# Two more groups of the second down block by seven products, their weight sums formed in HBM by adding transfers

## The chip, the cores and the metric

The kernel runs on one core of one Trainium2 chip. The metric is the device time of one execution in microseconds (us). The core has a matrix engine (PE, TensorE), a vector engine (DVE), a scalar engine (ACT), GpSimd (POOL), a sequencer that mostly issues transfers (SP), and 16 DMA engines which all queues share. On-chip memory (SBUF) and the matmul accumulators (PSUM, eight banks of 128 x 512 float32) are managed by hand; weights lie in HBM.

## The reference

One transformer block in float32 on 256 rows of width 2048: three kinds of attention side by side, gated and merged, then a feed-forward part. Cut to the part that matters here:

```python
x = x + merged @ w_out[l]
h2 = rms_norm(x, g_ffn[l])
u = causal_depthwise_conv(h2 @ w_up[l], conv_w[l], conv_b[l])   # 2048 -> 2 x 5632
u_gate, u_val = jnp.split(u, 2, axis=-1)
x = x + (jax.nn.silu(u_gate) * u_val) @ w_down[l]               # 5632 -> 2048
```

The last product, of the activations a = silu(u_gate) * u_val (256 x 5632) with w_down (5632 x 2048), is the "down" product. The change is there.

## The kernel before

**Float32 by three passes.** A float32 operand is split into a high part (`hi`, a rounded copy made by ACT) and a low part (`lo`, the rest, by DVE); `three` issues three matmuls, hi x hi, lo x hi, hi x lo. So each weight tile is loaded into a `raw` buffer by SP, cast by ACT into one of four `hi` buffers and subtracted by DVE into one of four `lo` buffers (`parts`, lines 354 and 355; `piece`, lines 142 to 144, does it in the up stage), then used by PE (lines 360 to 362, and 1289 and 1290 in the up stage). In the up stage `raw` has four buffers, in the down stage six that take turns (`raw_tile`), and two small ones (`junk`) for tiles of half size.

**Stages.** After attention, gates and the output product comes the up stage (h2 @ w_up): 11 rounds of four column tiles of the gate half (`s` = 0) and then the same four of the value half (`s` = 1), each over 16 row tiles, two at a time. A `tick()` follows each pair of row tiles: it advances generators that put side work into the program, among them the convolutions (`conv`, `taken`), which end in `split_to`, that writes an activation tile into `aT`. Generators in the list `background` are advanced first in each tick, and beside the up stage one of them, `pair_sums_ahead`, forms sums of weights.

**The down product by eight or by seven.** The down product runs as two blocks of 1024 output columns (`nb` 0 and 1, function `blocked`). A block goes over the 44 row tiles of w_down in 22 groups of two (a group is a pair `p` of tiles). For one group the product is a 2 x 2 block product: two halves of the rows of x (t), two row tiles of weights (j), two column halves of 512 (n). `eight(p)` makes the eight block products directly: two loads of 512 KB. `seven(p)` makes them by a scheme of Strassen's kind with seven: it needs sums of activations (`s_of`, four of them, S1 to S4) and sums of weights T1 to T4, where, with the weight blocks B00, B01 (first row tile) and B10, B11 (second), T1 = B00 + B01, T3 = B01 + B11, T2 = T1 + B11, T4 = T2 + B10. Y, four more PSUM banks, collects products that belong to more than one output; `gather` adds them up after the last seven of the block.

The plan of a block is a string in `d_plans`: `e` a group by eight, `s` the next group by seven, `f` a step `form()` that forms the sums of activations of one pair: DVE adds and subtracts into a scratch tile (lines 369 to 374), then ACT and DVE split the four results (lines 376 and 378). Groups by seven take pairs 0, 1, 2 and so on, groups by eight the remaining ones. The first block has 11 of each, and its sums of activations are used again in the second block; there pairs from 11 on need `f` steps of their own, and their sums are written over the activations of pairs that a group by eight has just used for the last time.

**The sums of weights** are formed ahead and kept in HBM: one DRAM tile of 128 x 4 x 512 per group (`kept_for`), with the places T1, T3, T4, T2 in that order. In the up stage `pair_sums_ahead` loads the 1 MB of a pair (`pre_d`, line 305), lets DVE add (lines 252 to 254, `sums_in`), and stores 1 MB (line 295). It starts 22 ticks into the stage (`DU`) and does a pair every eight ticks; the deque `halves` lists all sums to be formed. `seven` loads, on SP in this order, B00 and T3 into one raw tile (lines 447 and 448), B10 and B11 (line 416), T1 and T2 (line 451), and T4 into a `junk` tile (line 453).

**Order.** `in_order` (keep_in_program_order) pins instructions to program order on their engine. SP issues its transfers in program order, so one that waits for a buffer holds up all behind it. POOL does nothing in the up stage but two small transfers at its start, of row scales through HBM (`rstd_row`, `rbc`, lines 1160 and 1161).

Of the kernel before, what the change touches and what calls it, by code (L numbers as in the profile page):

```python
# [10 lines left out]
F32 = mybir.dt.float32  # L11
F32R = mybir.dt.float32r
AF = mybir.ActivationFunctionType
ALU = mybir.AluOpType
AX = mybir.AxisListType

P = 128
# [16 lines left out]
PIECE = 1024  # L34
# [9 lines left out]
def hybrid_block(  # L44
# [25 lines left out]
    nc = tc.nc  # L70
    nc.scalar.preload_act_table_set("natural_log_exp_and_others")

    cst = ctx.enter_context(tc.tile_pool(name="cst", bufs=1))
# [28 lines left out]
    background = []  # L102
# [72 lines left out]
    def split_to(dst, src):  # L175

        nc.scalar.copy(dst[..., :S], src)
        nc.vector.tensor_tensor(dst[..., S:], src, dst[..., :S].bitcast(F32), ALU.subtract)
# [25 lines left out]
    def k_tiles(name):  # L204
# [23 lines left out]
    g_plans = (("", "esesesee", "esesesee"), ("esesesee", "esesesee", "esesesee"))  # L228
    d_plans = (
        "efefefef" + "sef" * 4 + "ssefsfssfssee",  # L230
        "efefef" + "sss" + "esss" * 3 + "ssee",
    )
    T1, T3, T4, T2 = range(4)
    FS2, FS4, FS3, FS1 = range(4)
    in_order = tc.keep_in_program_order
    dram = ctx.enter_context(tc.tile_pool(name="dram", bufs=1, space=bass.MemoryType.DRAM))
    by_k = lambda w: w[0].rearrange("(k p) n -> p k n", p=P)
# [6 lines left out]
        for name, w, plans in (("o", w_out, o_plans), ("d", w_down, d_plans))  # L244
        for nb, plan in enumerate(plans)
        for pr in pairs(name, plan.count("s"))
        for h in range(2)
    )

    def sums_in(w):  # L250
        both = w[:, 1:2].to_broadcast([P, 2, w.shape[2]])
        in_order(nc.vector.tensor_tensor(w[:, 0:2], w[:, 0:4:3], both, ALU.add))
        in_order(nc.vector.tensor_tensor(w[:, T2], w[:, T1], w[:, T2], ALU.add))
        in_order(nc.vector.tensor_tensor(w[:, T4], w[:, T2], w[:, T4], ALU.add))

    def kept_for(name, nb, pr):
        if (name, nb, pr) not in sums_of:
            at = f"kept_{name}{nb}_{pr}"
            sums_of[name, nb, pr] = dram.tile([P, 4, 512], F32, tag=at, name=at)
        return sums_of[name, nb, pr]  # L260
# [24 lines left out]
    def pair_sums_ahead(staging, period, add, store, most=99, delay=0):  # L285

        due = deque()
        clock = 0
        for _ in range(delay):
            yield  # L290

        def step():
            while due and due[0][0] <= clock:
                _, kept, w = due.popleft()
                in_order(nc.sync.dma_start(kept, w))

        periods = cycle(period if isinstance(period, tuple) else (period,))
        while len(halves) > 1 and halves[0][-1] == 0 and most:
            most -= 1
            name, wv, nb, pr, _ = halves.popleft()  # L300
            halves.popleft()
            kept = kept_for(name, nb, pr)
            w = staging(f"pre_{name}{nb}_{pr}")
            in_order(
                nc.sync.dma_start(
                    w.rearrange("p (k c) -> p k c", k=2), wv[:, 2 * pr : 2 * pr + 2, nb * PIECE : (nb + 1) * PIECE]
                )
            )
            w = w.rearrange("p (i c) -> p i c", i=4)
            due.append((clock + store, kept, w))  # L310
            for t in range(next(periods)):
                if t == add:
                    sums_in(w)
                step()
                clock += 1
                yield
        while due:
            step()
            clock += 1
            yield  # L320

    def first_sums():

        name, wv, nb, pr, _ = halves.popleft()
        halves.popleft()
        kept = kept_for(name, nb, pr)
        two = []
        for h in range(2):
            w = block(f"pre_{name}{nb}_{pr}_{h}").rearrange("p (i c) -> p i c", i=4)
            two.append(w)  # L330
            n0 = nb * PIECE + h * 256
            for n in range(2):
                in_order(
                    nc.sync.dma_start(
                        w.rearrange("p (k n) c -> p k n c", k=2)[:, :, n],
                        wv[:, 2 * pr : 2 * pr + 2, n0 + n * 512 : n0 + n * 512 + 256],
                    )
                )
            yield
            yield  # L340
        for w in two:
            sums_in(w)
            yield
        for _ in range(3):
            yield
        for h, w in enumerate(two):
            in_order(nc.sync.dma_start(kept[:, :, h * 256 : (h + 1) * 256], w))
            yield
# [475 lines left out]
    def in_turn(name):  # L824
        turn[0] += 1
        return staged[:, turn[0] % 2]

    background.append(pair_sums_ahead(in_turn, PF, 3, 7, most=14))
    qm = heads_of(block("qm"))
    y = norm_heads(ps, rstd, "mq")  # L830
# [237 lines left out]
    for m in range(2):  # L1068
        gate = []
        for b, plan in enumerate(g_plans[m]):  # L1070
            g, bias = [], []
# [56 lines left out]
        for n in range(2):  # L1128
            acc = gate[branches[0][3]][n]
            for i, (w, k0, nk, b) in enumerate(branches):  # L1130
# [5 lines left out]
                for t in range(NT):  # L1136
                    g = gate[b][n]
# [41 lines left out]
    for nb, plan in enumerate(o_plans):  # L1179
# [20 lines left out]
    background.append(  # L1200
        pair_sums_ahead(lambda name: ends_tile(name, F32).rearrange("p i c -> p (i c)"), 8, 1, 5, delay=DU)
    )

    def a_pair(p):
        if p < FA // 2:
            return aT[:, 2 * p : 2 * p + 2]
        if not ends:
            ends.append(ends_tile("a_ends", F32R).rearrange("p i (k c) -> p i k c", k=2))
        return ends[0][:, p - FA // 2]
# [19 lines left out]
    def y_tile(f, s):  # L1229
        return cp.tile([P, S], F32, tag="y", bufs=6, name=f"y_{f}_{s}")  # L1230

    def taken(cr, y, f, s):
        ct = s * FT + f
        u = pads[f % 2]
        ins = nc.vector.tensor_tensor(u[:, 2:], cr, rbc, ALU.mult)  # L1235
        if y is not None:
            in_order(ins)
        y = y_tile(f, s) if y is None else y
        tap = lambda j: taps[:, j, ct : ct + 1]
        nc.scalar.activation(y, u[:, 2:], AF.Identity, scale=tap(2), bias=tap(3))  # L1240
        nc.vector.scalar_tensor_tensor(y, u[:, 1 : S + 1], tap(1), y, ALU.mult, ALU.add)
        nc.vector.scalar_tensor_tensor(y, u[:, 0:S], tap(0), y, ALU.mult, ALU.add)
        if s == 0:
            nc.scalar.activation(y, y, AF.Silu)
            ys[f] = y
        else:
            g = ys.pop(f)
            nc.vector.tensor_tensor(g, g, y, ALU.mult)
            split_to(a_pair(f // 2)[:, f % 2], g)

    def conv(ps, f, s):
        taken(out_of(ps, cp.tile([P, S], F32, tag="cr", bufs=2, name=f"cr_{f}_{s}")), None, f, s)
        return
        yield
# [19 lines left out]
    for f0 in range(0, FT, 4):  # L1274
# [5 lines left out]
        for s in range(2):  # L1280
            ps = [bank(f"u{f0 + i}_{s}") for i in range(4)]
            c0 = s * D_FF + f0 * P
            for k in range(0, KT, 2):
                hi, lo = piece(upv[:, k : k + 2, c0 : c0 + 512], 2, 512, f"u{f0}_{s}_{k}")
                for j in range(2):
                    first, last = k + j == 0, k + j == KT - 1
                    for i in range(4):
                        c = slice(i * P, (i + 1) * P)
# [23 lines left out]
    N0, N1 = (plan.count("s") for plan in d_plans)  # L1312
# [3 lines left out]
    a_blocks = aT.rearrange("p k (l t q) -> p k l t q", l=2, t=NT)  # L1316
    formed = [0]

    def s_of(p, f):


        if f == FS1:
            return a_blocks[:, 2 * p, :, 1]
        if p < 9:
            return sf[:, 3 * p + f]
        if p == 9:
            return sf_more[0][:, f] if f < 2 else sf_rest[2]
        if p == 10:
            return sf[:, 27] if f == 0 else sf_rest[f - 1]
        return a_blocks[:, 2 * (p - N0 + N1) + f // 2, :, f % 2]  # L1330

    tmp_d = lambda name: place([P, PIECE], F32, "ts", name)

    def form():
        p = formed[0]
        formed[0] += 1
        if p == 9:
            sf_rest.extend(cst.tile([P, 2, P], F32R, tag=tag, name=f"sf_{tag}") for tag in ("rbc", "taps", "rows"))
        if p < 9:
            groups = [(sf[:, 3 * p : 3 * p + 3], slice(0, 3))]  # L1340
        elif p == 9:
            sf_more.append(place([P, 2, 2, P], F32R, "sf", "sf_more"))
            groups = [(sf_more[0], slice(0, 2)), (sf_rest[2], 2)]
        else:
            groups = [(s_of(p, f), f) for f in range(3)]
        pair_sums(a_pair(p), tmp_d(f"fw_{p}"), groups + [(s_of(p, FS1), FS1)])
# [4 lines left out]
    for nb, plan in enumerate(d_plans):  # L1351
        apart = [] if nb == 1 else None
        X = blocked(
            "d", w_down, nb, nb * PIECE, plan, lambda p, j: a_pair(p)[:, j], s_of, raw_d, junk,
            lambda n0, Y: gather(n0, Y, tmp_d), None, form, apart,
        )
        for t in range(NT):
            for n in range(2):
                c = nb * PIECE + n * 512
                o = xres[:, t, c : c + 512]  # L1360
                nc.vector.tensor_tensor(o, o, X[t][n], ALU.add)
                if (nb, t, n) == (1, 1, 1):
                    nc.scalar.dma_start(ov[:, t, c : c + 256], o[:, :256])
                    c, o = c + 256, o[:, 256:]
                    nc.vector.tensor_tensor(o, o, apart[0], ALU.add)
                    nc.scalar.dma_start(ov[:, t, c : c + 256], o)
                else:
                    nc.scalar.dma_start(ov[:, t, c : c + 512], o)
# [31 lines left out]
```

## Time and profile before

| | us |
|---|---|
| median of 3 runs | 1460.83 |
| lowest, highest | 1460.07, 1462.5 |
| the profiled execution's own time | 1460.56 |
| its span, first to last instruction | 1458.8 |
| granted TensorE clock, share of full | 1.00 |

| stage | from, to (us in the span) | length |
|---|---|---|
| up | 757 to 1240 | 483 |
| down, first block | 1240 to 1344 | 104 |
| down, second block | 1344 to 1455 | 111 |

The profile is of one execution. A row of a group of instructions reads: line, engine, operation, output <- input, partitions x elements and type, count | busy us, mean ns of one | idle time of that engine just before, with what ended it. A row of a stage gives busy us and count for each engine, then the granted clock, the mean busy share of the 16 DMA engines and GB/s. Matmuls are pipelined and their ends are modelled: a matmul row's own length is longer than the distance to the next one. A wait reads: who waited <- for what: us in total, times, longest. "PE u L1289" is PE's matmul into `u` at line 1289.

### The profile page before, as it was taken

To read this page: it belongs to the slowest core of one execution; us is meant where nothing else is said; L and a number is where in the kernel's file an instruction comes from. 1 tells how busy PE (TensorE), PEld (TensorE's weight loads), DVE (VectorE), ACT (ScalarE), POOL (GpSimd) and SP (SyncE) were. 2 spreads that over 40 slices of the span, in tenths; PEclk is the share of its full clock that TensorE was granted. 3 is DMA by queue.
4 is the path that set the end of the run, shared out by engine and by line. 5 is a ranking of instruction groups with operands and counts; after the bars stand their busy time and mean duration, and the time that the engine had idled before them with its cause. 6 is when DMAs were issued, how large, how long until landed. Compare 5 with 4: busy or idle time off the path is not lost.

```text
span 1458.8 us, 20569 instructions
## 1 busy us (share of the span) xinstructions
PE 1452.1 (100%) x7295; PEld 1228.4 (84%) x7295; DVE 1221.8 (84%) x1804; ACT 851.9 (58%) x1210; POOL 21.4 (1%) x52
## 2 busy tenths in 40 slices
PE   9999999999999999999999999999999999999998
PEld 7888878888888888888888888888888888888887
DVE  5788778776898899998987888888888877999878
ACT  6755445464564555546766656556556565676665
POOL 0000010010000000000000000000000000000000
PEclk9999999999999999999999999999999999999999
DMA  8797899777668576788877888888888866789896
GB/s 290 228 352 247 320 323 333 266 250 217 212 206 268 176 226 201 271 266 261 304 213 231 290 275 299 282 270 299 286 278 298 272 197 201 253 283 341 293 334 220
DMA packets 166502, 387.64 MB, mean 266 GB/s; under 512 B 12554, under 2 KB 29854, under 8 KB 162174
## 3 DMA queue, kind: packets, MB, share of 16 engines
q1 hardware_dynamic: 164702, 383.29, 79.2%
q10 hardware_dynamic: 1328, 2.11, 0.4%
q8 instruction: 57, 0.93, 0.3%
q0 software_dynamic: 368, 0.93, 0.2%
q14 instruction: 47, 0.39, 0.1%
HBM read 347.47 MB, written 38.80 MB: 265 GB/s over the span
## 4 chain that ended last, share of the span: by engine, by line
PE 95%; issue 1%; DVE 1%; DMA 1%; SPq 0%; ACT 0%; POOL 0%; DVEq 0%; POOLq 0%; ACTq 0%
PE u L1289 22%; PE u L1290 11%; PE xg L362 4%; PE xg L361 4%; PE xg L360 4%; PE xd L360 4%; PE xd L362 3%; PE xd L361 3%; PE s L362 2%; PE f L360 2%; PE s L360 2%; PE f L362 2%; PE f L361 2%; PE b L362 2%; PE s L361 2%; PE b L361 2%
## 5 line engine op out<-in xcount | busy, mean ns | idle before, releaser
L1289 PE MATMUL u<-hT,hi_u 128*128 128x512 f32 x1232 | 428.5, 394 | 0.0
L1290 PE MATMUL u<-hT,lo_u 128*128 128x256 f32 x1232 | 341.5, 277 | 0.0
L1289 PEld LDWEIGHTS u<-hT,hi_u 128*128 128x128 f32 x1232 | 231.0, 188 | 53.4
L144 DVE TENSOR_TENSOR lo_u<-raw_u,hi_u 128x1024 fp32r<-128x1024 f32 x176 | 215.5, 1225 | 72.1 <-ACT hi_u L143 71.8
L143 ACT CAST hi_u<-raw_u 128x1024 fp32r<-128x1024 f32 x176 | 184.7, 1050 | 132.7 <-PE u L1289 107.0
L1290 PEld LDWEIGHTS u<-hT,lo_u 128*128 128x128 f32 x1232 | 231.5, 188 | 0.0
L355 DVE TENSOR_TENSOR lo_d<-raw_d,hi_d 128x1024 fp32r<-128x1024 f32 x88 | 106.8, 1223 | 16.7 <-ACT hi_d L354 14.3
L354 ACT CAST hi_d<-raw_d 128x1024 fp32r<-128x1024 f32 x88 | 91.8, 1053 | 39.9 <-PE xd L361 14.3
L354 ACT CAST hi_g<-raw_g 128x1024 fp32r<-128x1024 f32 (+1 forms) x80 | 77.0, 972 | 48.5 <-PE xg L361 19.2
L355 DVE TENSOR_TENSOR lo_g<-raw_g,hi_g 128x1024 fp32r<-128x1024 f32 (+1 forms) x80 | 88.7, 1121 | 4.1 <-ACT hi_g L354 4.1
L362 PE MATMUL xg<-lo_g,xT 128*128 128x512 f32 x175 | 68.1, 389 | 0.0
L360 PE MATMUL xg<-hi_g,xT 128*128 128x512 f32 x175 | 68.1, 389 | 0.0
L361 PE MATMUL xg<-hi_g,xT 128*128 128x512 f32 x175 | 68.1, 389 | 0.0
L143 ACT CAST hi_f<-raw_f 128x1024 fp32r<-128x1024 f32 (+1 forms) x40 | 38.5, 966 | 46.3 <-PE f L361 30.7
L144 DVE TENSOR_TENSOR lo_s<-raw_s,hi_s 128x1024 fp32r<-128x1024 f32 (+1 forms) x40 | 44.5, 1119 | 24.4 <-ACT hi_s L143 24.4
L1289 PE MATMUL u<-hT_rest,hi_u 128*128 128x512 f32 x176 | 62.0, 394 | 0.0
L143 ACT CAST hi_s<-raw_s 128x1024 fp32r<-128x1024 f32 (+1 forms) x40 | 38.4, 962 | 38.2 <-PE s L361 26.5
L143 ACT CAST hi_b<-raw_b 128x1024 fp32r<-128x1024 f32 x32 | 33.7, 1052 | 45.4 <-PE b L361 18.6
L1240 ACT ACTIVATE y<-u,taps 128x256 f32<-128x256 f32 x88 | 49.5, 595 | 17.0 <-DVE u L1235 16.8
L144 DVE TENSOR_TENSOR lo_f<-raw_f,hi_f 128x1024 fp32r<-128x1024 f32 (+1 forms) x40 | 44.4, 1117 | 16.9 <-ACT hi_f L143 16.9
L360 PE MATMUL xd<-hi_d,aT 128*128 128x512 f32 x148 | 57.6, 389 | 0.0
L362 PE MATMUL xd<-lo_d,aT 128*128 128x512 f32 x148 | 57.6, 389 | 0.0
(551 smaller groups left out, 3484.0 us busy)
## 6 DMA issues: line engine op xcount, KB each, us to landing
raw_u<-in_w_up_dram SPq DMA_DIRECT2D x176, 512.0 KB, 4.8
raw_g<-in_w_in_dram SPq DMA_DIRECT2D x96, 512.0 KB, 4.5
raw_d<-in_w_down_dram SPq DMA_DIRECT2D x63, 512.0 KB, 5.6
pre_d<-in_w_down_dram SPq DMA_DIRECT2D x17, 1024.0 KB, 7.2
kept_d<-pre_d SPq DMA_DIRECT2D x17, 1024.0 KB, 6.7
raw_f<-in_w_in_dram SPq DMA_DIRECT2D x32, 512.0 KB, 5.8
raw_s<-in_w_in_dram SPq DMA_DIRECT2D x32, 512.0 KB, 6.1
raw_t_d<-kept_d SPq DMA_DIRECT2D x25, 512.0 KB, 5.8
```

The source lines that it names most:

```text
L143: pin(nc.scalar.copy(hi[:, :m], raw[:, :m]))
L144: pin(nc.vector.tensor_tensor(lo[:, :m], raw[:, :m], hi[:, :m].bitcast(F32), ALU.subtract))
L354: nc.scalar.copy(hi[:, :n], src)
L355: nc.vector.tensor_tensor(lo[:, :n], src, hi[:, :n].bitcast(F32), ALU.subtract)
L360: fix(nc.tensor.matmul(o, lhsT=ah, rhs=w[0], start=first, stop=False))
L361: fix(nc.tensor.matmul(o, lhsT=al, rhs=w[0], start=False, stop=False))
L362: fix(nc.tensor.matmul(o, lhsT=ah, rhs=w[1], start=False, stop=last))
L1240: nc.scalar.activation(y, u[:, 2:], AF.Identity, scale=tap(2), bias=tap(3))
L1289: nc.tensor.matmul(ps[i], lhsT=hi[:, j, c], rhs=hT(k + j), start=first, stop=False)
L1290: nc.tensor.matmul(ps[i][:, :S], lhsT=lo[:, j, c], rhs=hT(k + j)[:, :S], start=False, stop=last)
```

## The change

The second block's plan goes from 14 groups by seven and 8 by eight, with 3 `f` steps, to 16 and 6, with 5, in another order. The sums of weights of the two new groups, pairs 14 and 15, are not formed by `pair_sums_ahead` (its list leaves them out, and is the same 25 pairs as before for w_down), but by a new background generator of the up stage. It waits until an activation tile is being written, lets POOL copy one column of it (so that POOL waits for it on the chip), then issues on POOL a copy of the pair's 1 MB of weights from HBM into the kept tile and four transfers of 256 KB that add onto it in HBM, each of which needs the one before or the copy; 40 ticks later the same for the second pair. The places in which sums of activations of pairs 11 to 15 are kept move to the activations of pairs 16 to 19, packed without gaps.

```diff
@@ -228,8 +228,9 @@
     g_plans = (("", "esesesee", "esesesee"), ("esesesee", "esesesee", "esesesee"))
     d_plans = (
         "efefefef" + "sef" * 4 + "ssefsfssfssee",
-        "efefef" + "sss" + "esss" * 3 + "ssee",
+        "efsss" * 3 + "efssfsssssee",
     )
+    in_hbm = [("d", 1, pr) for pr in range(14, 16)]
     T1, T3, T4, T2 = range(4)
     FS2, FS4, FS3, FS1 = range(4)
     in_order = tc.keep_in_program_order
@@ -244,6 +245,7 @@
         for name, w, plans in (("o", w_out, o_plans), ("d", w_down, d_plans))
         for nb, plan in enumerate(plans)
         for pr in pairs(name, plan.count("s"))
+        if (name, nb, pr) not in in_hbm
         for h in range(2)
     )
 
@@ -318,6 +320,21 @@
             step()
             clock += 1
             yield
+
+    def sums_in_hbm(period):
+        mark = cst.tile([P, 1], F32, tag="rows", name="mark")
+        for name, nb, pr in in_hbm:
+            while not a_done:
+                yield
+            in_order(nc.gpsimd.tensor_copy(mark, a_done[-1][:, :1].bitcast(F32)))
+            kept = kept_for(name, nb, pr)
+            b = by_k(w_down)[:, 2 * pr : 2 * pr + 2, nb * PIECE : (nb + 1) * PIECE]
+            b = b.rearrange("p k (n c) -> p k n c", n=2)
+            in_order(nc.gpsimd.dma_start(kept.rearrange("p (k n) c -> p k n c", k=2), b))
+            for dst, src in ((0, b[:, 0, 1]), (1, b[:, 1, 1]), (3, kept[:, 0]), (2, kept[:, 3])):
+                in_order(nc.gpsimd.dma_start(kept[:, dst], src, accum_op=ALU.add))
+            for _ in range(period):
+                yield
 
     def first_sums():
 
@@ -1200,6 +1217,8 @@
     background.append(
         pair_sums_ahead(lambda name: ends_tile(name, F32).rearrange("p i c -> p (i c)"), 8, 1, 5, delay=DU)
     )
+    a_done = []
+    background.append(sums_in_hbm(40))
 
     def a_pair(p):
         if p < FA // 2:
@@ -1246,7 +1265,8 @@
         else:
             g = ys.pop(f)
             nc.vector.tensor_tensor(g, g, y, ALU.mult)
-            split_to(a_pair(f // 2)[:, f % 2], g)
+            a_done.append(a_pair(f // 2)[:, f % 2])
+            split_to(a_done[-1], g)
 
     def conv(ps, f, s):
         taken(out_of(ps, cp.tile([P, S], F32, tag="cr", bufs=2, name=f"cr_{f}_{s}")), None, f, s)
@@ -1327,7 +1347,8 @@
             return sf_more[0][:, f] if f < 2 else sf_rest[2]
         if p == 10:
             return sf[:, 27] if f == 0 else sf_rest[f - 1]
-        return a_blocks[:, 2 * (p - N0 + N1) + f // 2, :, f % 2]
+        i = 3 * (p - N0) + f
+        return a_blocks[:, 2 * N1 + i // 2, :, i % 2]
 
     tmp_d = lambda name: place([P, PIECE], F32, "ts", name)
 
```

## Prediction

> **What bounds the kernel now.** I read the summary first, then the chain of waits, then busy time by stage, because a share of the whole span hides which engine limits which stage.
>
> ```profile
> span 1458.8 us, 20569 instructions
> PE 1452.1 (100%) x7295; PEld 1228.4 (84%) x7295; DVE 1221.8 (84%) x1804; ACT 851.9 (58%) x1210; POOL 21.4 (1%) x52
> PE 95%; issue 1%; DVE 1%; DMA 1%; SPq 0%; ACT 0%; POOL 0%; DVEq 0%; POOLq 0%; ACTq 0%
> ```
>
> PE is the whole chain: the rest of it is 5%. Busy time alone does not prove that PE never waits, so the next view counts its matmuls in stages. The columns are the engines' busy time and instructions, granted clock, share of the 16 DMA engines, and GB/s.
>
> ```profile
> 757.00:1240.00 483.00, 483.00 (x2778) 422.18 (x2777) 402.79 (x661) 287.16 (x440) 1.29 (x2) 1.00 0.81 266
> 1250.00:1450.00 200.00, 200.00 (x884) 165.62 (x883) 179.19 (x237) 132.49 (x167) 0.00 (x0) 1.00 0.87 298
> 1240.00:1344.00 104.00, 104.00 (x461) 86.08 (x460) 99.85 (x151) 69.92 (x92) 0.00 (x0) 1.00 0.86 293
> 1344.00:1455.00 111.00, 110.85 (x495) 91.87 (x493) 92.67 (x110) 68.26 (x82) 0.00 (x0) 1.00 0.84 287
> 1370.00:1400.00 30.00, 30.00 (x134) 24.84 (x133) 23.67 (x22) 19.45 (x21) 0.00 (x0) 1.00 0.98 340
> 1414.00:1440.00 26.00, 26.00 (x116) 21.52 (x115) 20.37 (x19) 17.97 (x20) 0.00 (x0) 1.00 1.00 350
> ```
>
> 757 to 1240 us is the up stage, 1240 to 1344 the first down block, 1344 to 1455 the second. Over 200 us of the down stage 884 matmuls are counted, two of them cut by the edges: 200 / 882 = **0.227 us each**. The timeline gives the same for neighbours, so this is the undisturbed pace and the stage has no stalls to win back:
>
> ```profile
> 1439.43 0.39 PE L362 MATMUL yd<-lo_d,aT 128*128 128x512 f32 x1
> 1439.65 0.39 PE L360 MATMUL yd<-hi_d,aT 128*128 128x512 f32 x1
> 1439.88 0.39 PE L361 MATMUL yd<-hi_d,aT 128*128 128x512 f32 x1
> ```
>
> (The 0.39 is the pipelined length; the price of one more matmul is the step, 0.227.) The transfers are the other thing to see: 0.98 and 1.00 of the DMA engines are busy in the runs of sevens, at 340 to 350 GB/s.
>
> **What the change removes.** Two of the second block's 22 groups go from `eight` to `seven`. An eight issues 2 x 2 x 2 x 3 = 24 matmuls of 512 columns, a seven 7 x 3 = 21. Six go: 6 x 0.227 = **-1.36 us**, all on the path. That is also the most it can give, since nothing else on PE changes.
>
> **What it adds on VectorE and ScalarE in the second block.** By form, these are the rows (count, then busy us and mean ns):
>
> ```profile
> L355 DVE TENSOR_TENSOR lo_d<-raw_d,hi_d 128x1024 fp32r<-128x1024 f32 x42 | 51.1, 1224 | 9.2 <-ACT hi_d L354 7.3
> L355 DVE TENSOR_TENSOR lo_t_d<-raw_t_d,hi_t_d 128x512 fp32r<-128x512 f32 x14 | 9.6, 689 | 3.4 <-ACT hi_t_d L354 3.4
> L354 ACT CAST hi_d<-raw_d 128x1024 fp32r<-128x1024 f32 x41 | 43.0, 1053 | 19.3 <-PE xd L361 5.7 <-PE yd L361 5.6 <-DVE fw L369 3.9
> L369 DVE TENSOR_TENSOR fw<-aT 128x512 f32<-128x512 f32 x3 | 2.1, 690 | 0.0
> L372 DVE TENSOR_TENSOR fw<-fw 128x256 f32<-128x256 f32 x3 | 1.3, 422 | 0.0
> L373 DVE SCALAR_TENSOR_TENSOR fw<-fw 128x128 f32<-128x128 f32 x3 | 0.9, 293 | 0.1
> L374 DVE TENSOR_TENSOR fw<-fw 128x128 f32<-128x128 f32 x3 | 0.9, 286 | 0.0
> L378 DVE TENSOR_TENSOR aT<-fw,aT 128x128 fp32r<-128x128 f32 x12 | 2.7, 285 | 0.0
> ```
>
> A seven splits 3.5 tiles (3 x 1.224 + 0.689 = 4.36 us of DVE), an eight two (2.45): +1.91 twice, 3.8. Two more `f` steps cost 0.690 + 0.422 + 0.293 + 0.286 + 4 x 0.285 = 2.83 each, 5.7. DVE goes from 92.7 to about 102 us in a block of 109 us, 94%. The first block already runs at 99.85 of 104 us (96%) with 461 matmuls, the same 0.227, so this is covered by PE; I cost it at nothing. ACT has far more room (68.3 of 111; two casts of 1.053 become three and a half). Uncovered, the 9.5 us of DVE would be the price.
>
> **The new order.** The first seven comes after one eight instead of three, so its four PSUM banks, those of the first block's X, must be free 24 x 0.227 = 5.4 us after the stage's start at 1344, by 1349.4. The adds that free them end at 1345.45:
>
> ```profile
> 1342.98 2.47 DVE L1361 TENSOR_TENSOR xres_again<-xres_again,xd 128x512 f32<-128x512 f32 x4
> ```
>
> Four us are left, so nothing is paid. An `f` still stands behind the eight whose activations it overwrites, as before.
>
> **Transfers in the second block.** Issue, size, and median us to landing:
>
> ```profile
> raw_u<-in_w_up_dram SPq DMA_DIRECT2D x176, 512.0 KB, 4.8
> pre_d<-in_w_down_dram SPq DMA_DIRECT2D x17, 1024.0 KB, 7.2
> kept_d<-pre_d SPq DMA_DIRECT2D x17, 1024.0 KB, 6.7
> raw_t_d<-kept_d SPq DMA_DIRECT2D x25, 512.0 KB, 5.8
> raw_d<-kept_d SPq DMA_DIRECT2D x25, 256.0 KB, 5.2
> rstd_row<-scales POOLq DMA_DIRECT2D x1, 1.0 KB, 9.9
> ```
>
> A seven loads 256 + 256 + 512 + 512 + 256 KB = 1.835 MB in five issues, an eight 1.049 MB in two. On SP that is six more issues, behind whose waits only the following loads stand. A seven takes 21 x 0.227 = 4.77 us of PE and 1.835 MB / 340 GB/s = 5.40 us of DMA: each seven in a row falls **0.63 us** behind, each eight (5.45 against 3.09) gains 2.4. The longest run was five sevens (3.2 us behind), the new one has seven of them, with an `f` inside (4.4 us): 1.3 us later at its end. How near the edge the old run is, the block's waits say (total us, times, longest):
>
> ```profile
> ACT hi_d L354 <- PE xd L361: 5.7, 14, 1.7
> ACT hi_d L354 <- DMA raw_d<-kept_d: 0.8, 1, 0.8
> ACT hi_d L354 <- DMA raw_d<-in_w_down_dram: 0.8, 3, 0.4
> ```
>
> ACT mostly waits for PE to give a hi tile back, and only four times, by 0.4 to 0.8 us, for a landing. Behind that stand the tiles already split: when a hi tile comes free three others of 6 x 0.227 = 1.36 us are full, 4.1 us, less cast and subtraction (1.05 + 1.22), leaves 1.8 us of cover. 1.3 more plus 0.4 is just inside it; earlier, the first three sevens meet the first block's 1 MB of output (3 us of DMA time), but after three eights in a row. Bounds: 0 to +3 us (cover gone and 340 falling to 325); I take +0.3, nearer to the covered end.
>
> The Trainium skill (DMA: Bandwidth & Descriptors, section Specifications) gives about 358 GB/s of HBM per core. By it a seven would fall 0.36 us behind, the run of seven 2.5 us, and the 0.3 of the sum below would be nothing; the trace's 340 to 350 at a full share is below it, and decides.
>
> **Sums formed by POOL in the up stage.** Per group: a tiny copy on POOL that waits for an activation tile, a 1 MB copy HBM to HBM, four adding transfers of 256 KB, each behind the landing of the one before. Behind them on POOL stands nothing: it has two instructions from 757 to 1240 us and none later. The sums are loaded after 1400 us, so the chain's length is free. What can cost is the share of the 16 engines. No row shows an adding transfer. Low bound: every byte once, 2.1 MB at 266 / 0.81 = 328 GB/s: 6.4 us per group, over a chain of 6.7 + 4 x 5.2 = 27 us in which 0.19 x 27 = 5.1 us are spare. High bound: reads and writes each counted, 2.1 + 3.15 = 5.2 MB, 16 us, over 7.2 + 6.7 + 4 x 9.9 = 53 us with 10 us spare (5 if the chain stays short). So the weight loads would come 1 to 11 us late at worst. Their cover:
>
> ```profile
> ACT hi_u L143 <- PE u L1289: 103.4, 90, 1.7
> ACT hi_u L143 <- DMA raw_u<-in_w_up_dram: 8.5, 3, 5.6
> POOL rbc L1161 <- DMA rstd_row<-scales: 9.5, 1, 9.5
> DMA to landing us min/median/max: 9.9/10.8/11.6
> ```
>
> A tile feeds 8 matmuls of 512 and 8 of 256 columns: 483 / 2776 x 16 = 2.78 us. When ACT gets a hi tile back (90 times) three are full, 8.3 us, less 2.3 for the split: 6 us. The four raw buffers add 4 x 2.78 - 2.3 - 4.8 - 0.4 = 3.6 us. Together **9 us** or so. The last row above is of raw_u loads issued from 757 to 780 us, beside POOL's rstd_row transfer: 10.8 instead of 4.8 us, and ACT waited up to 5.6 us; yet PE kept its pace, which confirms the cover. I take the low bound, since the new pieces are rows of 2 KB like the loads': 0. Gains are excluded here: nothing is taken away in this stage.
>
> **Sum.** The profiled execution took 1460.56 us (1.8 around the span); - 1.36 + 0.3 = 1459.5. The median of the three runs lies 0.27 above it, so I forecast **1459.8**.
>
> **Rivals.**
> - *Loads bind the second block* (for: 0.98 and 1.00 shares, four late landings; against: no PE gap, only 1.3 us more). PE stalls 1 to 3 us at the end of the run of seven sevens: - 1.36 + 2, **1461.5**.
> - *The adding transfers hold up the weight loads* (slower). Place: from the first activation tile on, about 795 us by the row below, and again 40 ticks of 2.78 us later. For: the rstd_row row, 6 us of lateness from 1 KB, and a chain gives no 20 us to recover. Against: that transfer was 4-byte pieces. It decides once a chain's five transfers make loads late by over 9 us, 1.8 each. At 3 us each it is (15 - 9) x 2 = 12 us: **1471**; at 6 each 42 us.
>
> ```profile
> 794.67 0.41 ACT L177 CAST aT<-y 128x256 fp32r<-128x256 f32 x1 [0.20 <-DVE y L1248]
> ```
>
> - *No gain*: an `f` or a late bank eats the six matmuls: **1460.8**.
>
> The same page of the Trainium skill (Specifications) says that below 512 B the engines read, modify and write. The rstd_row row agrees, and by that alone the new 2 KB pieces would be harmless; its Rules for kernel authors add that an accumulate reads its destination and writes it later, whatever the size, which no row here shows.
>
> **How the numbers follow.** Forecast 0.66, loads bind 0.15, adding transfers 0.15, no gain 0.04. A measurement of this kernel can tell about 0.2% (2.9 us) from nothing, more than the whole gain, so forecast and no gain count as within; so do nearly all of loads bind. Within 0.80; slower 0.17 (0.15 and 0.02 of loads bind); faster 0.03, for a shift that I do not see. The range goes from 1458.5 (the full 1.36 under the lowest run, 1460.07, is 1458.7) to 1464.2 (loads bind at its bound of +3, under the highest run, 1462.5); it leaves out the adding transfers' case and a few hundredths.
>
> **What would show it.** 7289 matmuls; 0.227 us still between them in both down blocks; in the second, ACT waiting a little longer for raw_d and kept_d; in the up stage, ACT's waits for raw_u above 8.5 us at about 800 and 910 us, with 16 matmuls per 2.78 us kept. Wrong if PE has gaps near 800 to 960 us (adding transfers) or 1400 to 1445 us (loads).

## The result and the profile after

| us | before | after |
|---|---|---|
| median of 22 executions | 1460.76 | 1465.84 |
| lowest, highest | 1459.73, 1462.5 | 1458.59, 1469.11 |
| the profiled execution | 1460.56 | 1459.05 |

The ratio of after to before is 1.0024, with a 95% interval of 1.0013 to 1.0035: slower, by 5.1 us in the medians, where 1.0 us faster was forecast, with a chance of 0.80 for a change within 0.2% and a range that ended at 1464.2 us. One number cannot tell what happened, though. The 22 times lie in **two groups**: 7 from 1458.59 to 1460.66 us, where the forecast had them, and 15 from 1463.32 to 1469.11. Before there is one group. The profile after is of the quick group. Its summary, and the POOL queue's row (packets, MB, share of the 16 DMA engines):

```profile
span 1457.3 us, 20637 instructions
PE 1451.0 (100%) x7289; PEld 1227.9 (84%) x7289; DVE 1227.3 (84%) x1824; ACT 857.8 (59%) x1222; POOL 30.9 (2%) x64
q0 software_dynamic: 2064, 5.12, 1.5%
```

The six matmuls are gone (7289) and the span is 1.5 us shorter. POOL's queue was at 0.2% before; the 1.3% more of 1457 us, over two chains, is about 9.5 us of all 16 engines for each chain, between the 6.4 and 16 of the bounds. The stages (us of the span; columns as before):

```profile
795.00:835.00 40.00, 40.00 (x232) 34.96 (x232) 34.60 (x57) 23.56 (x36) 4.92 (x6) 1.00 0.96 311
850.00:1200.00 350.00, 350.00 (x2021) 306.05 (x2021) 298.97 (x492) 208.17 (x319) 4.55 (x6) 1.00 0.85 283
1250.00:1450.00 200.00, 200.00 (x884) 165.59 (x883) 187.36 (x260) 137.57 (x178) 0.00 (x0) 1.00 0.88 306
1344.00:1455.00 111.00, 109.30 (x488) 90.55 (x486) 100.14 (x131) 73.52 (x94) 0.00 (x0) 1.00 0.87 306
```

In the down stage 884 matmuls in 200 us is the count of before, so the new plan costs no stall, and DVE's 100.1 us is close to the 102 worked out. In the up stage PE keeps its pace too, but the cover is being used. These are the waits of that stage (who waited <- for what: us, times, longest):

```profile
ACT hi_u L143 <- PE u L1309: 69.8, 70, 1.7
ACT hi_u L143 <- DMA raw_u<-in_w_up_dram: 43.2, 24, 5.7
```

ACT waited for landings 24 times instead of 3, 43.2 us instead of 8.5. In this execution that stayed just inside the cover.

### The profile page after: what moved, and what is told of

The parts are those of the page before. It is cut to its first block, busy times and chain, and to the rows that moved or that the text cites. A ratio compares the mean times of both kernels' runs of the same rounds, so it can differ in the third digit from the quotient of the medians.

```text
span 1457.3 us, 20637 instructions
## 1 busy us (share of the span) xinstructions
PE 1451.0 (100%) x7289; PEld 1227.9 (84%) x7289; DVE 1227.3 (84%) x1824; ACT 857.8 (59%) x1222; POOL 30.9 (2%) x64
## 4 chain that ended last, share of the span: by engine, by line
PE 98%; issue 1%; DVE 0%; DMA 0%; POOL 0%; POOLq 0%; DVEq 0%
PE u L1309 22%; PE u L1310 11%; PE xg L379 4%; PE xg L377 4%; PE xg L378 4%; PE xd L378 3%; PE xd L377 3%; PE xd L379 3%; PE s L379 2%; PE f L377 2%; PE s L377 2%; PE f L379 2%; PE f L378 2%; PE s L378 2%; PE b L377 2%; PE b L379 2%
## 5 line engine op out<-in xcount | busy, mean ns | idle before, releaser
L371 ACT CAST hi_t_d<-raw_t_d 128x1024 fp32r<-128x1024 f32 (+1 forms) x54 | 43.5, 835 | 19.4 <-PE xd L378 12.4
L371 ACT CAST hi_t_g<-t_g 128x1024 fp32r<-128x1024 f32 x30 | 31.5, 1051 | 39.2 <-PE xg L378 35.9
```

What stands on the lines that cost most here:

```text
L371: nc.scalar.copy(hi[:, :n], src)
```

## The experiments

Two theories stood at the start. A: POOL's chains make the up stage's weight loads late beyond their cover. B: the second down block is bound by its loads. Each run also timed the kernel before beside it, its median between 1460.07 and 1460.56 us. The changed kernel itself was executed only twice more, for traces, so how often a kernel comes out long is compared between executions that were not taken side by side.

**The changed kernel again, for a trace.** No edit.

> The changed kernel as it is, for a second trace. Its 22 executions lie in two groups, 7 from 1458.6 to 1460.7 us and 15 from 1463.3 to 1469.1, and the trace at hand is one of the first group (1459.05, PE without a gap from 757 us on). Theory A (POOL's chain of transfers makes the up stage's weight loads late beyond their cover): a trace of the second group has 4 to 9 us of PE gaps between 795 and 960 us and none in the down blocks. Theory B (the second down block is bound by its loads): the gaps stand between 1400 and 1445 us. A trace of the first group would tell nothing new but the cover left, about 0.5 us at the tightest place.

It took 1458.33 us, a quick one again: it told nothing of the long group.

**The plan alone, the chain alone, the copy alone.** `...` stands for lines left out. In the first, the two new groups load plain weights in the place of their sums.

```diff
 # plan_alone
-    background.append(sums_in_hbm(40))
 ...
+            plain = (name, nb, p) in in_hbm
+            kept = wv[:, 2 * p : 2 * p + 2, n0 : n0 + PIECE] if plain else sums_of[name, nb, p]
 ...
 # chain_alone
-        "efsss" * 3 + "efssfsssssee",
+        "efefef" + "sss" + "esss" * 3 + "ssee",
 # copy_only
-            for dst, src in ((0, b[:, 0, 1]), (1, b[:, 1, 1]), (3, kept[:, 0]), (2, kept[:, 3])):
-                in_order(nc.gpsimd.dma_start(kept[:, dst], src, accum_op=ALU.add))
```

> The new plan of 16 groups by seven, without POOL's chain: the two new groups load plain weights of the same sizes where their sums would be (the output of these two groups is therefore not the reference's). Theory A: 1459.4 us, 1.4 under the kernel before, in every execution, no second group. Theory B: still two groups, median 1464 to 1467.

> POOL's chain of transfers as in the changed kernel, with the old plan of 14 groups by seven (the two sums are formed and not used). Theory A: two groups of times, the fast one at 1460.6 to 1461, the slow one at 1465 to 1470, median about 1467 (1.4 over the changed kernel's 1465.8). Theory B: 1460.8 us like the kernel before, in every execution.

> The changed kernel without the eight adding transfers: POOL copies the two pairs' weights, 1 MB each, and nothing is added (so the two groups work with plain weights). If the adding transfers are what makes the loads late: 1459.4 us in every execution. If the two copies of 1 MB suffice: two groups of times, median well over 1461 us.

The kernel before had a median of 1460.3 us beside them.

| us | median | lowest, highest | over 1463 |
|---|---|---|---|
| plan alone | 1458.97 | 1457.88, 1460.68 | 0 of 11 |
| chain alone | 1461.26 | 1458.84, 1467.5 | 4 of 12 |
| copy alone | 1459.53 | 1458.23, 1460.09 | 0 of 11 |

Theory B falls: without the chain there is one group, and by the medians the plan is worth 1.3 us (ratio 0.9991, 0.9982 to 1.0, so just at the edge of the noise). The chain alone makes the long group, though in fewer executions than expected, and the copies alone, with half as many bytes written, do not. The same wait in the up stage, of the chain alone and then of the copy alone, both in quick executions:

```profile
ACT hi_u L143 <- DMA raw_u<-in_w_up_dram: 34.7, 18, 5.3
```

```profile
ACT hi_u L143 <- DMA raw_u<-in_w_up_dram: 17.1, 9, 5.8
```

From 795 to 830 us, beside the first chain, the slowest raw_u load landed after 10.2 us in the profile after and after 10.1 with the chain alone, but after 5.4 with the copy alone and 5.8 in the kernel before.

**The changed kernel once more, and four chains.**

```diff
 # chain_four
-        for name, nb, pr in in_hbm:
+        for i, (name, nb, pr) in enumerate(in_hbm * 2):
 ...
+            if i < 2:
+                kept = dram.tile([P, 4, 512], F32, tag=f"spare_{i}", name=f"spare_{i}")
 ...
-    background.append(sums_in_hbm(40))
+    background.append(sums_in_hbm(20))
```

> The changed kernel once more, for a trace of the slow group. Theory A: 4 to 9 us of PE gaps between 795 and 960 us, none in the down blocks. Of the fast group: PE without gaps from 757 us on.

> The changed kernel with four of POOL's chains in place of two, one each 20 ticks instead of 40; the first two go to spare places in HBM that nothing reads. Theory A (the chain makes weight loads late until PE runs dry): with the cover used up by each chain before it can recover, every execution is slow, 1465 to 1485 us, and the trace has PE gaps beside the chains, between 795 and 960 us, with ACT waiting for raw_u just before each. Theory C (the slow group is some state of the chip that the chain only triggers now and then, and no backlog): still two groups, the fast one at 1459.4.

The changed kernel's execution fell in the long group, 1467.77 us, and its trace is the key to the case. First POOL's first chain in it (start, length, instruction, idle before):

```profile
794.48 0.67 POOL L333 DMA_DIRECT2D kept_d<-in_w_down_dram  x1
803.90 1.75 POOL L335 DMA_DIRECT2D kept_d<-in_w_down_dram  x2 [8.75 <-DMA kept_d<-in_w_down_dram]
813.54 0.81 POOL L335 DMA_DIRECT2D kept_d<-kept_d  x1 [7.88 <-DMA kept_d<-in_w_down_dram]
823.32 0.81 POOL L335 DMA_DIRECT2D kept_d<-kept_d  x1 [8.97 <-DMA kept_d<-kept_d]
```

Two adding transfers go out together at 804 us, since each needs only the copy, and beside them SP issues the 1 MB store of other sums at 805. Two raw_u loads follow at 806.5 and 808.0 us. The profile knows the landing of the second (us to landing: min/median/max), and ACT stands still for the first:

```profile
DMA to landing us min/median/max: 14.4/14.4/14.4
```

```profile
819.15 1.05 ACT L143 CAST hi_u<-raw_u 128x1024 fp32r<-128x1024 f32 x1 [6.64 <-DMA raw_u<-in_w_up_dram]
```

The second landed after 14.4 us instead of 4.8, 9.6 late. The first was cast 12.7 us after its issue, some 8 late, and PE stopped for its low part. The prediction had put the cover at 9 us. PE's own rows show the stop, and something else behind it:

```profile
820.56 0.40 PE L1309 MATMUL u<-hT,hi_u 128*128 128x512 f32 x1
820.79 0.28 PE L1310 MATMUL u<-hT,lo_u 128*128 128x256 f32 x1
820.91 0.39 PE L1309 MATMUL u<-hT,hi_u 128*128 128x512 f32 x1
821.51 0.39 PE L1310 MATMUL u<-hT,lo_u 128*128 128x256 f32 x1 [0.21 <-DVE lo_u L144]
821.73 0.39 PE L1309 MATMUL u<-hT,hi_u 128*128 128x512 f32 x1
...
822.79 0.40 PE L1309 MATMUL u<-hT,hi_u 128*128 128x512 f32 x1
```

The stop is short, 821.51 - 820.91 = 0.60 us where 0.23 is the rule. But after it three pairs of a 512- and a 256-column matmul take 822.79 - 821.73 = 1.06 us, 353 ns a pair, where the trace of before has 347. Three more stops follow, and each can change the pace again. The second, the stretch behind it, then the fourth with its stretch:

```profile
824.80 0.39 PE L1310 MATMUL u<-hT,lo_u 128*128 128x256 f32 x1 [0.20 <-DVE lo_u L144]
825.02 0.39 PE L1309 MATMUL u<-hT,hi_u 128*128 128x512 f32 x1
...
829.88 0.39 PE L1309 MATMUL u<-hT,hi_u 128*128 128x512 f32 x1
...
833.43 0.39 PE L1309 MATMUL u<-hT,hi_u 128*128 128x512 f32 x1
833.77 0.39 PE L1310 MATMUL u<-hT,lo_u 128*128 128x256 f32 x1
833.99 0.39 PE L1309 MATMUL u<-hT,hi_u 128*128 128x512 f32 x1
...
840.35 0.40 PE L1309 MATMUL u<-hT,hi_u 128*128 128x512 f32 x1
```

From 825.02 to 829.88 us 14 pairs take 347 ns each: the second stop had brought the quicker pace back, and the third, at 830.8 us, left it. From 833.99 to 840.35 us 18 pairs take 353 ns each, and so it stays. The fourth stop, which set this pace, is a delay of only 0.11 us (833.77 - 833.43 = 0.34, where 0.23 is the rule). Counted over long stretches of this trace:

```profile
795.00:835.00 40.00, 39.44 (x223) 33.58 (x222) 30.43 (x49) 21.24 (x33) 3.52 (x5) 1.00 0.92 276
850.00:1200.00 350.00, 350.00 (x1983) 303.57 (x1982) 294.40 (x478) 204.19 (x314) 4.54 (x6) 1.00 0.84 282
1250.00:1450.00 200.00, 200.00 (x884) 165.56 (x883) 187.13 (x263) 140.23 (x183) 0.00 (x0) 1.00 0.92 316
```

From 795 to 835 us there are nine matmuls fewer than in the profile after (223 to 232): some 1.6 us of stops. From 850 to 1200 us there are 1983 instead of 2021, **1.9% fewer, with PE busy all the time**, the granted clock at 1.00 and ACT long back to waiting for PE. Without the two at the edges, 350 us / 990.5 pairs is 353.4 ns, and 350 / 1009.5 is 346.7. The down stage has its 884 again. This span is 8.7 us longer than that of the profile after: some 1.6 us are the stops, and the slower pace over the 407 us from 834 us to the stage's end costs 7.6; against that the stage had begun 0.6 us earlier.

The four chains took 1469.17 to 1476.44 us in all four executions. Three stretches of the trace:

```profile
850.00:915.00 65.00, 65.00 (x370) 56.40 (x369) 52.73 (x88) 36.99 (x59) 13.18 (x11) 1.00 0.96 317
930.00:980.00 50.00, 50.00 (x290) 44.10 (x289) 43.73 (x76) 29.34 (x47) 9.48 (x6) 1.00 0.96 329
1000.00:1200.00 200.00, 200.00 (x1134) 173.50 (x1133) 166.90 (x268) 116.27 (x178) 0.00 (x0) 1.00 0.83 276
```

Pairs of 353 ns, then of 347 (50 / 144), then of 353 (200 / 566). Between the first two stand two stops:

```profile
919.92 0.28 PE L1312 MATMUL u<-hT,lo_u 128*128 128x256 f32 x1
921.80 0.50 PE L1311 MATMUL u<-hT_rest,hi_u 128*128 128x512 f32 x1 [1.61 <-ACT hi_u L143]
923.07 0.39 PE L1312 MATMUL u<-hT_rest,lo_u 128*128 128x256 f32 x1 [0.77 <-DVE lo_u L144]
```

Here too stops led from the slower pace back to the quicker, while the DMA engines were at 0.96 on both sides. A stop of 0.6 us at 985 us brought the slower pace back, and the first slower stretch had begun at 821.3 us behind a delay of only 0.07 us. That is against pace as an effect of the transfers' load, and made theory S: a stop of PE, from whatever cause, draws one of two paces for the matmuls that follow.

**Chains that are spread or late.**

```diff
 # spaced
+            wait = lambda: in_order(nc.gpsimd.tensor_copy(mark, a_done[-1][:, :1].bitcast(F32)))
 ...
             for dst, src in ...
+                for _ in range(12):
+                    yield
+                wait()
                 in_order(nc.gpsimd.dma_start(kept[:, dst], src, accum_op=ALU.add))
 ...
-    background.append(sums_in_hbm(40))
+    background.append(sums_in_hbm(12))
 # late
         mark = cst.tile([P, 1], F32, tag="rows", name="mark")
+        for _ in range(150):
+            yield
 ...
-    background.append(sums_in_hbm(40))
+    background.append(sums_in_hbm(2))
```

> The changed kernel with each of the ten POOL transfers waiting for an activation of its own, 12 ticks (33 us) further on, so that no two adding transfers are under way together; the same bytes. Theory A by the density of the chain (a share of 0.99 for 35 us): one group at 1459.4 us. If a single adding transfer is enough to make PE run dry: slow executions stay, 1463 and more in a third or more of them.

> The changed kernel with both chains at the end of the up stage: the generator starts after 150 ticks, when the loads and stores of the other sums are done (about 1165 us on), 2 ticks between the two. There the share of the DMA engines was 0.54 to 0.74 before. Theory A: one group at 1459.4 us, 1.4 under the kernel before, in every execution. If the adding transfers disturb by themselves, whatever else is under way: slow executions stay.

Spaced: median 1459.14 us, ten of eleven up to 1461.9 and one at 1464.22, so density seems to be most of it, but one long execution in eleven leaves open whether a single adding transfer can suffice. In its trace the slowest raw_u load from 795 to 830 us landed after 5.2 us. Late: median 1459.19, none over 1460.58, by the medians 1.37 us under the 1460.56 beside it (0.9994, 0.9985 to 1.0003, so not clear of noise). By theory S this does not prove that late chains never stop PE: with some 75 us of the stage left, the slower pace would cost 1.4 us at most.

**A stop without any chain.** The kernel before, and one stop put into PE's stream:

```diff
+    gap = cst.tile([P, P], mybir.dt.bfloat16, name="gap")
+    nc.gpsimd.memset(gap, 0.0)
 ...
+            if (f0, s) == (8, 0):          # gap_late: (36, 0)
+                for i in range(2):
+                    if i:
+                        in_order(nc.gpsimd.memset(gap, 0.0))
+                    in_order(nc.tensor.matmul(ps[3][:, :384], lhsT=gap, rhs=idle[:, :384], start=True, stop=True))
```

> The kernel before, with none of the change, and one short stop of PE in the up stage: at its third round (tick 32, about 845 us) two matmuls on zeros, the second of which waits for POOL to rewrite its weights. The trace of the slow group has PE gaps of 1.6 us in all at 821 to 834 us, and after them two matmuls (512 and 256 columns) take 353.3 ns instead of 346.7 until the stage ends. Theory S (a stop of PE, whatever its cause, can change the pace of the stage's remaining matmuls by 1.9%): two groups of times, one at about 1461.5 (the stop and two matmuls, 1 us), one at 399 us x 0.019 = 7.7 us more, 1469; the trace has 346.7 or 353.3 ns throughout after the stop. Theory A as it stood (the chain's transfers cost the time themselves, by late loads): one group at 1461 to 1462, and 346.7 ns.

> The same stop in the tenth of the eleven rounds (tick 144, about 1155 us). Theory S: what the slower pace costs goes with what is left of the stage, 89 us x 0.019 = 1.7 us, so 1461.5 or 1463.2. Theory A as it stood: 1461 to 1462 as for the early stop.

The early stop: ten of twelve from 1459.75 to 1462.52 us, two at **1468.44 and 1469.51**. The profile is of the first of these two. The stop in it, and the stretch behind it:

```profile
832.64 0.34 PE L1290 MATMUL u<-idle,gap 128*128 128x384 bf16 x1
832.68 0.52 PE L1297 MATMUL u<-hT,hi_u 128*128 128x512 f32 x1
833.04 0.28 PE L1298 MATMUL u<-hT,lo_u 128*128 128x256 f32 x1
833.30 0.34 PE L1290 MATMUL u<-idle,gap 128*128 128x384 bf16 x1
```

```profile
850.00:1200.00 350.00, 350.00 (x1983) 303.57 (x1982) 291.84 (x475) 203.63 (x312) 0.00 (x0) 1.00 0.80 273
```

1983 matmuls, the count of the long execution, in a kernel without the chain and without the plan, and POOL idle; before the stop, from 757 to 832 us, its pairs took 346.7 ns. That shows the core of theory S: a stop alone can bring the slower pace. (The first of the two inserted matmuls is followed by one of the stage before the second is issued; the stop is there all the same, as three delays of 0.13 us each.) The late stop lay between 1459.9 and 1462.63 us, median 1461.2: nothing near 1468, as it must be with 89 us of stage left, but its 1.7 us cannot be told from noise. In its trace the same insertion, at 1142 us, left the pace at 346.7 ns.

**A stop behind the chains, and the late chains again.** The edit of gap_early at `(16, 0)` in the changed kernel; late again unchanged.

> The changed kernel with the short stop of PE (two matmuls on zeros, the second behind POOL) added at tick 64, about 935 us, just behind the second chain. Of 12 executions of the kernel before with such a stop, two went on at the slower pace and ten at 346.7 ns. Theory S (a stop draws the pace anew, and a draw seldom gives the slower one): most executions that the chains made slow go back to 346.7 ns at 935 us; they pay the slower pace for at most 110 us (2.1 us), so most times lie between 1460 and 1463 us, and at most a fifth near 1467; median about 1461.5, under the 1465.8 of the changed kernel though work is added. Theory A' (the slower pace belongs to what the chains left behind, not to the stop): times as of the changed kernel, 1 us more, two thirds of them at 1464 to 1470.

> The changed kernel with both chains after tick 150, once more, as the version to keep: 1459.2 us, 1.36 under the kernel before, and no execution above 1461.

With the stop added, ten of eleven executions were at 1459.11 to 1460.88 us and one at 1467.68, where the changed kernel, timed apart from them, had 15 of 22 long ones. The median, 1459.81, is even under the 1461.5 expected, so the run fits theory S, but it does not show that the stop turned slow executions back. One that the first chain had made slow would have paid 1.6 us (from 834 to 921 us, where the inserted stop lay), besides its stops, and few of the ten can have done so. Whether the others had been made slow by the second chain just before and were turned back, or were quick all along, their times do not tell. The one trace is quick, with 346.7 ns on both sides of the stop; a turning back was seen in the traces of the long execution and of the four chains. The late chains gave 1458.60 us against 1460.48, ratio 0.9988 (0.9979 to 0.9997), none over 1460.07. In that trace the chains run from 1157 to about 1210 us; that stretch, and the two waits:

```profile
1157.00:1210.00 53.00, 53.00 (x308) 46.32 (x307) 40.55 (x67) 30.50 (x46) 9.20 (x12) 1.00 0.96 285
```

```profile
ACT hi_u L143 <- PE u L1311: 99.3, 90, 1.8
ACT hi_u L143 <- DMA raw_u<-in_w_up_dram: 13.0, 7, 4.8
```

The share beside the chains is 0.96 here too (0.71 in the kernel before), and the slowest raw_u load beside them landed after 10.9 us; but the last store of other sums goes out at 1160 us, before the first adding transfer, ACT waits for landings 7 times instead of 24, and PE does not stop. This time the late version is faster than the kernel before by more than the noise, and of its 22 executions in the two runs none is over 1460.58.

## Why the prediction was wrong

- **-1.36 us for six matmuls: borne out.** The plan alone is worth 1.34 us by the medians (by the interval 0 to 2.6), and the quick group's trace 1.5.
- **DVE, banks, forms and loads of the second block (+0.3): right as far as the traces go, even a little high; the times cannot tell 0.3 from nothing.** No matmul is missing in the down stage, in either group. The one long wait for a landing in the second block (4.0 us, for sums of weights) stood at the first seven, not at the end of the run of seven.
- **The adding transfers, taken at 0: wrong, and this is the step that failed.** The low bound was chosen "since the new pieces are rows of 2 KB like the loads'". The chain's engine time was about 9.5 us instead of 6.4, and, more to the point, the sum took the four transfers one behind the other and spread them evenly over a chain of 27 to 53 us. In fact they fell in lumps: the first two need only the copy and go out together, and beside them and a 1 MB store one load came some 8 us late and the next 9.6, just beyond the cover. The cover itself, 9 us, was sized about right. In the kernel before the same store stands there, and no load took over 5.8 us. The Trainium skill (DMA: Bandwidth & Descriptors, section Issuing engines are not separate DMA queues) says that transfers of all issuing engines interleave on the same 16 DMA engines; the trace agrees: beside POOL's transfers one of SP's loads took 14.4 us, where their median is 4.8.
- **The price of lateness: wrong in kind.** The rival took the lateness beyond the cover as the cost, (15 - 9) x 2 = 12 us if every transfer made loads 3 us late, and got 0.15. The time came out between the forecast and its 1471, but not by its sum. Shown instead, in the trace of the long group: lateness just beyond the edge, stops of 1.6 us in all, and then 1.9% on every matmul up to the end of the stage, 7.6 us. Where a stop can cost that much however short it is, an edge that is reached in some executions is to be priced at that amount, with its chance.
- The signs named for this case (waits for raw_u at about 800 and 900 us, gaps in PE) were the right place to look; "16 matmuls per 2.78 us kept" was true only in the quick group.

What stays open: why a pair takes 346.7 or 353.3 ns, what in a stop decides it, and why the chains made 15 of 22 executions long in the changed kernel, 4 of 12 without the plan and, with the stop added, 1 of 11, all timed apart from each other. Only one long execution of the changed kernel has a trace; that the 15 of the 22 went the same way is inferred from their times. Whether adding transfers weigh more than plain ones of the same bytes and place was not measured by itself.

## What to carry to other kernels

A stream of matmuls that never stops has a cover to be kept, not a spare to be spent: before adding transfers beside it, find the tightest moment, with what else is in flight then, instead of a mean share. Put background transfers where the queue is emptier and a stop would cost least (here the last 80 us of the stage, with a share of 0.71 before instead of 0.87), even if their result is needed much later. And time more than one or two executions: the one profile at hand, of the quick group, showed nothing but 1.5 us gained.

## What the runs showed of the hardware

The pace of an unbroken stream of matmuls (512 and 256 columns in turn, each with its weight load) has two steady values, 346.7 and 353.3 ns a pair, at the same granted clock of 1.00. It changed only at stops in these traces, and a delay of 0.07 us was enough. The slower pace followed the stops at 821.5 and 833.8 us of the long execution, those at 821.3 and 985 us with four chains, and the inserted one at 832 us. The quicker came back after the stops at 824.8 us of the long execution and at 920 to 923 us with four chains. The pace stayed quick after the inserted stops at 921 and 1142 us. Of twelve executions with one inserted stop two were long; no trace here shows the two values in the down stage, whose matmuls are all of 512 columns.

An adding transfer of 256 KB within HBM landed in 5.1 to 13.9 us, where a plain load of 256 KB has a median of 5.2, and a chain of one copy and four of them took 29 to 35 us in the traces of the changed kernel.
